# Seven products for eight in part of the down projection of a two-layer encoder kernel

## The chip, the cores and the metric

One core of a Trainium2 chip runs the kernel. The metric is the device time of one execution, in microseconds; three runs of the kernel before gave 2172.10, 2170.59 and 2173.06.

## What is computed

Two layers over 256 tokens of width 2048, in float32, and a final normalisation. Each layer has a token mixer and then a gated feed-forward block (the FFN), in which most of the time lies; the change is in the FFN alone.

```
def _conv_ffn(h, w_up, conv_w, conv_b, w_down):
    s = h.shape[1]
    up = h @ w_up
    padded = jnp.pad(up, ((0, 0), (CONV_WIDTH - 1, 0), (0, 0)))
    c = conv_b + sum(conv_w[j] * padded[:, j:j + s] for j in range(CONV_WIDTH))
    a, g = jnp.split(c, 2, axis=-1)
    return (jax.nn.silu(g) * a) @ w_down
```

`w_up` is 2048 x 11264 and `w_down` 5632 x 2048 in each layer.

## The kernel before

Every large product is made from float32 weights in three TensorE terms: a weight tile is split into a rounded part `hi` and a remainder `lo`, the activations likewise, and hi x hi, hi x lo and lo x hi are summed in PSUM. `load_split` (L240) does this for the weights. It loads 1 MB (four k-tiles of 128 x 512) into a `raw` tile by one DMA on SyncE's queue (L250), and then for each piece of 1024 columns (two k-tiles) ScalarE casts `hi` (L258) and VectorE subtracts to get `lo` (L259). There are three `raw` buffers and five each of `hi` and `lo`, so a piece can be prepared once TensorE has finished with the piece five before it.

The FFN (`ffn`, L384) goes through its 44 tiles of 128 hidden columns in groups of 8, 12, 12 and 12 (`GROUPS`, L30). In a group, for every four hidden tiles, `fm_panel` (L266) is run for the first half of the up projection and again for the gating half: 64 pairs of matmuls, one of 512 and one of 256 columns, into four PSUM banks. `branch` (L391) then forms the convolution of each of the four tiles: ScalarE L285, VectorE L286, GpSimd L287, ScalarE L401, VectorE L403 and L405. `gate` (L410) adds SiLU (ScalarE L413), the product with the first half (VectorE L414), and the split of the activation into `h` (ScalarE L416, GpSimd L417). Panels of the next weights run on TensorE while a branch or gate is worked off on the other engines.

After a group's panels `residual` (L321) multiplies its hidden tiles with the rows of `w_down` in four chunks n of 512 output columns. `tm_chunk` (L296) takes for each k-tile and each half of the tokens three matmuls of 512 columns (L292 to L294) into one PSUM bank per half; a group of 12 makes 72 matmuls a chunk. VectorE then adds both banks to the running `x_sb` (L326). In the last group of layer 1 the final two tiles are left to `final` (L332). The pools that matter: six PSUM banks `acc`, ten small tiles `w15`, six `m4`, six `k2`.

The order on each engine is set by a planner when the program is built: of the instructions that it takes to be ready, the one that stands first in the program goes first on its engine. On the chip each engine then runs its list in that order.

## Time and profile before

| | us |
|---|---|
| three runs, median | 2172.1 |
| profiled execution, its own time | 2171.22 |
| span of its profile, first to last instruction | 2169.4 |
| TensorE busy | 2155.6 (99%) |
| VectorE busy | 1428.6 (66%) |
| ScalarE busy | 1126.2 (52%) |
| GpSimd busy | 341.1 (16%) |

The span is what the hardware profiler saw of one execution; the time of that execution is 1.8 us longer, and lies between the lowest and the middle of the three runs. In the profile PE is TensorE (PEld its weight loads), DVE VectorE, ACT ScalarE, POOL GpSimd and SP SyncE. A matmul's record holds its whole passage through the array, so records overlap; the distance from start to start tells the rate. An idle time in brackets stands ahead of its instruction and names what ended it.

### The profile page before, as it was taken

Reading aid. Unit: us, or ns where it says so; the run is one execution under the profiler, and the core shown is the slowest. Engines: PE = TensorE matmul, PEld = TensorE weight load, DVE = VectorE, ACT = ScalarE, POOL = GpSimd, SP = SyncE. Lnnn points to the kernel's source line nnn. Section 1 sums busy time; section 2 is a strip of 40 time slices with the busy share of each in tenths; the row PEclk is TensorE's granted clock in tenths of the full one; section 3 lists DMA queues with packets and bytes.
Section 4 is the critical chain, followed back from the end, with each engine's and each line's share of the span. In section 5 each row is a group of like instructions: output and inputs, shape, how many; then the busy total and the mean of one; then the engine's idle time right before and its main releaser. Section 6 shows DMA issues by size and latency. Waiting matters only on the chain.

```text
span 2169.4 us, 29090 instructions
## 1 busy us (share of the span) xinstructions
PE 2155.6 (99%) x11301; PEld 1851.1 (85%) x11301; DVE 1428.6 (66%) x1796; ACT 1126.2 (52%) x1658; POOL 341.1 (16%) x537
## 2 busy tenths in 40 slices
PE   9999999999999999999999999999999999999998
PEld 7888888888888888888888888888888888888886
DVE  5655555687676578577756555558767758765875
ACT  6545545464554456355554445446545535544654
POOL 0110120031221033022103000002212202210320
PEclk9999999999999999999999999999999999999999
DMA  9655565556556555556655555555656655665553
GB/s 319 212 175 190 164 200 186 175 194 200 188 194 197 192 195 192 196 175 209 202 176 180 185 177 194 189 180 188 200 176 204 203 189 184 202 201 184 186 193 137
DMA packets 209965, 416.77 MB, mean 192 GB/s; under 512 B 7036, under 2 KB 10404, under 8 KB 209828
## 3 DMA queue, kind: packets, MB, share of 16 engines
q1 hardware_dynamic: 208676, 412.27, 57.6%
q10 hardware_dynamic: 1152, 2.65, 0.3%
q8 instruction: 88, 1.44, 0.3%
q14 instruction: 49, 0.40, 0.0%
HBM read 412.80 MB, written 2.89 MB: 192 GB/s over the span
## 4 chain that ended last, share of the span: by engine, by line
PE 98%; DMA 1%; DVE 0%; issue 0%; ACT 0%; SPq 0%; POOLq 0%; POOL 0%; DVEq 0%
PE fm_u L273 29%; PE fm_u L276 15%; PE tm_d L294 7%; PE tm_d L293 7%; PE tm_d L292 7%; PE tm_oab L292 1%; PE fm_kb L273 1%; PE tm_oab L294 1%; PE tm_oab L293 1%; PE tm_ocd L292 1%; PE tm_ocd L294 1%; PE tm_ocd L293 1%; PE fm_qa L273 1%; PE fm_qb L273 1%; PE fm_ka L273 1%; PE tm_va L292 1%
## 5 line engine op out<-in xcount | busy, mean ns | idle before, releaser
L259 DVE TENSOR_TENSOR lo<-raw,hi 128x1024 fp32r<-128x1024 f32 (+1 forms) x770 | 1009.4, 1328 | 589.0 <-ACT hi L258 584.8
L258 ACT CAST hi<-raw 128x1024 fp32r<-128x1024 f32 (+1 forms) x770 | 791.4, 1046 | 674.9 <-PE tm_d L294 205.2
L273 PE MATMUL fm_u<-x_n,hi 128*128 128x512 f32 x2816 | 958.8, 389 | 0.0
L276 PE MATMUL fm_u<-x_n,lo 128*128 128x256 f32 x2816 | 777.3, 276 | 0.0
L273 PEld LDWEIGHTS fm_u<-x_n,hi 128*128 128x128 f32 x2816 | 528.6, 188 | 110.0
L276 PEld LDWEIGHTS fm_u<-x_n,lo 128*128 128x128 f32 x2816 | 528.6, 188 | 0.4
L287 POOL TENSOR_TENSOR u<-hf_u,row_n 128x256 f32<-128x256 f32 x176 | 170.7, 970 | 920.9 <-DVE hf_u L286 913.3
L292 PE MATMUL tm_d<-hi,h 128*128 128x512 f32 x688 | 268.0, 390 | 0.0
L293 PE MATMUL tm_d<-lo,h 128*128 128x512 f32 x688 | 267.8, 389 | 0.0
L294 PE MATMUL tm_d<-hi,h 128*128 128x512 f32 x688 | 267.7, 389 | 0.0
L401 ACT ACTIVATE c<-u,conv 128x256 f32<-128x256 f32 x176 | 106.0, 602 | 206.5 <-POOL u L398 204.5
L294 PEld LDWEIGHTS tm_d<-hi,h 128*128 128x128 f32 x688 | 129.1, 188 | 26.9
L292 PEld LDWEIGHTS tm_d<-hi,h 128*128 128x128 f32 x688 | 129.2, 188 | 26.8
L293 PEld LDWEIGHTS tm_d<-lo,h 128*128 128x128 f32 x688 | 129.2, 188 | 26.5
L403 DVE SCALAR_TENSOR_TENSOR c<-u,conv,c 128x256 f32<-128x256 f32 x176 | 84.0, 477 | 71.8 <-ACT c L401 71.7
L417 POOL TENSOR_TENSOR h<-c,h 128x256 fp32r<-128x256 f32 x88 | 89.8, 1020 | 145.7 <-ACT h L416 145.7
L405 DVE SCALAR_TENSOR_TENSOR c<-u,conv,c 128x256 f32<-128x256 f32 x176 | 97.0, 551 | 0.3
L286 DVE TENSOR_TENSOR hf_u<-fm_u,hf_u 128x256 f32<-128x256 f32 x176 | 73.1, 415 | 0.0
L285 ACT COPY hf_u<-fm_u 128x256 f32<-128x256 f32 x176 | 62.8, 357 | 6.2 <-PE fm_u L276 3.1
L413 ACT ACTIVATE c<-c 128x256 f32<-128x256 f32 x88 | 36.7, 417 | 45.0 <-DVE c L405 44.5
L414 DVE TENSOR_TENSOR c<-c,c 128x256 f32<-128x256 f32 x88 | 48.5, 552 | 7.9 <-ACT c L413 7.8
L126 POOL TENSOR_TENSOR rstd_n<-s_n,mhalf 128x2 f32<-128x2 f32 x4 | 2.8, 695 | 306.9 <-DVE s_n L180 306.9
(277 smaller groups left out, 2373.4 us busy)
## 6 DMA issues: line engine op xcount, KB each, us to landing
raw<-in_ffn_w_up_dram SPq DMA_DIRECT2D x176, 1024.0 KB, 5.0
raw<-in_ffn_w_down_dram SPq DMA_DIRECT2D x86, 1024.0 KB, 5.1
raw<-in_ab_w_in_dram SPq DMA_DIRECT2D x47, 1024.0 KB, 5.1
raw<-in_cd_w_in_dram SPq DMA_DIRECT2D x40, 1024.0 KB, 5.1
raw<-in_ab_w_out_dram SPq DMA_DIRECT2D x16, 1024.0 KB, 5.1
raw<-in_cd_w_out_dram SPq DMA_DIRECT2D x16, 1024.0 KB, 5.1
x_sb<-in_x_dram SPq DMA_DIRECT2D x4, 512.0 KB, 12.4
raw<-in_ffn_w_down_dram SPq DMA_DIRECT2D x4, 512.0 KB, 3.8
```

The source lines that it names most:

```text
L258: nc.scalar.copy(hi[:, b:b + size], raw[:, j + b:j + b + size])
L259: nc.vector.tensor_tensor(lo[:, b:b + size], raw[:, j + b:j + b + size], hi[:, b:b + size].bitcast(F32), ALU.subtract)
L273: nc.tensor.matmul(banks[m], hi[k][:, m * P:(m + 1) * P], xr, start=(k0 + k == 0), stop=False, skip_group_check=True)
L276: nc.tensor.matmul(banks[m][:, :T], lo[k][:, m * P:(m + 1) * P], xr[:, :T], start=False, stop=(k0 + k == KT - 1), skip_group_check=True)
L287: nc.gpsimd.tensor_tensor(dst, half, row, ALU.mult)
L292: nc.tensor.matmul(bank, xh, hi, start=st, stop=False)
L293: nc.tensor.matmul(bank, xh, lo, start=False, stop=False)
L294: nc.tensor.matmul(bank, xl, hi, start=False, stop=sp)
L401: nc.scalar.activation(c, u[:, 2:], AF.Identity, bias=cb[:, fi:fi + 1], scale=w2[:, fi:fi + 1])
L403: nc.vector.scalar_tensor_tensor(c, u[:, 1:T + 1], w1[:, fi:fi + 1], c, ALU.mult, ALU.add)
L405: nc.vector.scalar_tensor_tensor(c, u[:, :T], w0[:, fi:fi + 1], c, ALU.mult, ALU.add)
L417: nc.gpsimd.tensor_tensor(h[:, 1, :], c, h[:, 0, :].bitcast(F32), ALU.subtract)
```

## The change

In `residual`, chunks 0, 2 and 3 of a group of 12 (all such groups but the last of layer 1: five groups, 15 chunks) are made by a new `down_chunk`. Its first and last four k-tiles are done as before. The middle four are two pairs of k-tiles; each pair, with both token halves and both halves of the 512 output columns, is a 2 x 2 block product, which `seven` makes from seven products of 256 columns instead of eight, by Strassen's scheme. The sums of weights it needs are made by `load_forms`: four VectorE sums over 512 elements, one in place and three into a second `raw` tile, then the split of 1024 and 768 columns per pair. The sums of activations are made once per group, by `pair_forms`, inside the gate of the group's second four tiles. The products are accumulated in the chunk's two banks and two more (`sums`), and `combine` adds those from `sums` to `x_sb`, by one ScalarE copy and seven VectorE operations. Chunk 1, groups of 8 and the last group stay with `tm_chunk`.

```diff
@@ -318,9 +318,98 @@
                         pump()
         return banks
 
-    def residual(w, parts, norm, name):
+    def load_forms(src):
+        cnt[0] += 1
+        i = cnt[0]
+        raw = wp.tile([P, 2048], F32, tag="raw", name=f"raw{i}")
+        more = wp.tile([P, 2048], F32, tag="raw", name=f"more{i}")
+        nc.sync.dma_start(
+            raw.rearrange("p (k f) -> p k f", k=4), src.rearrange("(k p) f -> p k f", p=P))
+        v = raw.rearrange("p (q j n c) -> p q j n c", q=2, j=2, n=2)
+        b11, b12, b21, b22 = (v[:, :, j, n] for j in range(2) for n in range(2))
+        t3, t2, t4 = (
+            more[:, :1536].rearrange("p (q f c) -> p q f c", q=2, f=3)[:, :, f] for f in range(3))
+        nc.vector.tensor_tensor(t3, b12, b22, ALU.add)
+        nc.vector.tensor_tensor(b12, b11, b12, ALU.add)
+        nc.vector.tensor_tensor(t2, b12, b22, ALU.add)
+        nc.vector.tensor_tensor(t4, t2, b21, ALU.add)
+        quads = []
+        for q in range(2):
+            forms = []
+            for j, (part, m) in enumerate(((raw, 1024), (more, 768))):
+                hi = wp.tile([P, 1152], F32R, tag="hi", name=f"hi{i}_{q}{j}", bufs=5)[:, :m]
+                lo = wp.tile([P, 1024], F32R, tag="lo", name=f"lo{i}_{q}{j}", bufs=5)[:, :m]
+                pv = part[:, q * m:(q + 1) * m]
+                nc.scalar.copy(hi, pv)
+                nc.vector.tensor_tensor(lo, pv, hi.bitcast(F32), ALU.subtract)
+                forms += [(hi[:, b:b + 256], lo[:, b:b + 256]) for b in range(0, m, 256)]
+            quads.append(forms)
+        return quads
+
+    def seven(banks, sums, xs, rs, forms, first, last):
+        rh, rl = rs
+        a11, a21 = ((xs[0][:, 0, t * P:(t + 1) * P], xs[0][:, 1, t * P:(t + 1) * P]) for t in range(2))
+        a12, a22 = ((xs[1][:, 0, t * P:(t + 1) * P], xs[1][:, 1, t * P:(t + 1) * P]) for t in range(2))
+        r5, r6, r7, r3 = ((rh[:, f * P:(f + 1) * P], rl[:, f * P:(f + 1) * P]) for f in range(4))
+        b11, t1, b21, b22, t3, t2, t4 = forms
+        for dst, (ah, al), (bh, bl), own in (
+                (sums[0][:, :256], a11, b11, True), (sums[1][:, :256], r5, t1, True),
+                (banks[0][:, :256], a12, b21, False), (banks[0][:, 256:], r3, b22, False),
+                (sums[1][:, 256:], r7, t3, False), (sums[0][:, 256:], r6, t2, False),
+                (banks[1][:, :256], a22, t4, False)):
+            nc.tensor.matmul(dst, ah, bh, start=own and first, stop=False, skip_group_check=True)
+            nc.tensor.matmul(dst, ah, bl, start=False, stop=False, skip_group_check=True)
+            nc.tensor.matmul(dst, al, bh, start=False, stop=last, skip_group_check=True)
+
+    def combine(sums, n, name):
+        c = n * 512
+        x11, x21 = (x_sb[:, t, c:c + 256] for t in range(2))
+        p1 = w15(f"p1_{name}", 256)
+        nc.scalar.copy(p1, sums[0][:, :256])
+        w = w15(f"pw_{name}", 256)
+        nc.vector.tensor_tensor(w, sums[0][:, 256:], p1, ALU.subtract)
+        e = w15(f"pe_{name}", 256)
+        nc.vector.tensor_tensor(e, sums[1][:, :256], w, ALU.add)
+        nc.vector.tensor_tensor(x11, x11, p1, ALU.add)
+        nc.vector.tensor_tensor(x21, x21, w, ALU.subtract)
+        nc.vector.tensor_tensor(x21, x21, sums[1][:, 256:], ALU.subtract)
+        xb = x_sb[:, :, c + 256:c + 512]
+        nc.vector.tensor_tensor(xb, xb, e.unsqueeze(1).to_broadcast([P, 2, 256]), ALU.add)
+        nc.vector.tensor_tensor(xb[:, 1], xb[:, 1], sums[1][:, 256:], ALU.add)
+
+    def down_chunk(w, r0, xs, nk, rs, n, name):
+        banks = [acc(f"tm_{name}{t}") for t in range(2)]
+        sums = [acc(f"tms_{name}{t}") for t in range(2)]
+        for k0 in range(0, nk, 4):
+            kn = min(4, nk - k0)
+            src = w[r0 + k0 * P:r0 + (k0 + kn) * P, n * 512:n * 512 + 512]
+            if k0 == 4:
+                quads = load_forms(src)
+                for q in range(2):
+                    k = k0 + 2 * q
+                    seven(banks, sums, xs[k:k + 2], rs[q], quads[q], q == 0, q == 1)
+                    pump()
+                combine(sums, n, name)
+                continue
+            hi, lo = load_split(src, kn)
+            for k in range(kn):
+                a = xs[k0 + k]
+                for t in range(2):
+                    xh, xl = (a[:, j, t * P:(t + 1) * P] for j in range(2))
+                    for j, (s, m) in enumerate(((xh, hi[k]), (xh, lo[k]), (xl, hi[k]))):
+                        nc.tensor.matmul(
+                            banks[t], s, m, start=k0 + k + j == 0, stop=False, skip_group_check=True)
+                if k % 2 == 1:
+                    pump()
+        return banks
+
+    def residual(w, parts, norm, name, rs=None):
         for n in range(4):
-            banks = tm_chunk(w, parts, n * 512, f"{name}{n}")
+            if not rs or n == 1:
+                banks = tm_chunk(w, parts, n * 512, f"{name}{n}")
+            else:
+                (r0, xs, nk), = parts
+                banks = down_chunk(w, r0, xs, nk, rs, n, f"{name}{n}")
             for t in range(2):
                 xc = x_sb[:, t, n * 512:(n + 1) * 512]
                 nc.vector.tensor_tensor(xc, banks[t], xc, ALU.add)
@@ -407,32 +496,49 @@
                 cs.append(c)
                 yield m, c
 
-        def gate(kt0, cs, banks):
+        def pair_forms(c0, c1, nm):
+            r = m4(f"r{nm}")[:, :512]
+            r5, r6, r7, r3 = (r[:, f * P:(f + 1) * P] for f in range(4))
+            nc.vector.tensor_tensor(r5, c0[:, P:], c1[:, P:], ALU.subtract)
+            nc.vector.tensor_tensor(r6, c0[:, :P], r5, ALU.subtract)
+            nc.vector.tensor_tensor(r7, c0[:, P:], c0[:, :P], ALU.subtract)
+            nc.vector.tensor_tensor(r3, c1[:, :P], r6, ALU.subtract)
+            rh, rl = (
+                kp.tile([P, 512], F32R, tag="k2", name=f"r{j}{nm}", bufs=6) for j in range(2))
+            nc.scalar.copy(rh, r)
+            nc.vector.tensor_tensor(rl, r, rh.bitcast(F32), ALU.subtract)
+            return rh, rl
+
+        def gate(kt0, cs, banks, rs=None):
             nm = f"{layer}_{kt0}"
+            prev = None
             for m, c in branch(kt0, 1, banks):
                 nc.scalar.activation(c, c, AF.Silu)
                 nc.vector.tensor_tensor(c, cs[m], c, ALU.mult)
                 h = act(f"h{m}{nm}")
                 nc.scalar.copy(h[:, 0, :], c)
                 nc.gpsimd.tensor_tensor(h[:, 1, :], c, h[:, 0, :].bitcast(F32), ALU.subtract)
+                if rs is not None and m % 2 == 1:
+                    rs.append(pair_forms(prev, c, f"{nm}{m}"))
+                prev = c
                 yield h
 
         f0 = 0
         early = None
         for gi, gs in enumerate(GROUPS):
-            hs = []
+            hs, rs = [], []
             last = gi == len(GROUPS) - 1
             for kt0 in range(f0, f0 + gs, 4):
                 cs = early or [c for _, c in branch(kt0, 0, panel(kt0, 0))]
                 early = None
-                hs += gate(kt0, cs, panel(kt0, 1))
+                hs += gate(kt0, cs, panel(kt0, 1), rs if gs == 12 and not (last and nxt is None) and kt0 == f0 + 4 else None)
             if gs < 12:
                 early = [c for _, c in branch(f0 + gs, 0, panel(f0 + gs, 0))]
             if last and nxt is None:
                 residual(down, ((f0 * P, hs, gs - 2),), None, f"d{layer}{gi}")
                 final(down, (f0 + gs - 2) * P, hs[gs - 2:])
             else:
-                residual(down, ((f0 * P, hs, gs),), nxt if last else None, f"d{layer}{gi}")
+                residual(down, ((f0 * P, hs, gs),), nxt if last else None, f"d{layer}{gi}", rs)
             f0 += gs
 
     def heads_to_act(src, hd, name):
```

## Rows read from the trace of the kernel before

**Rows 1.** The page: each engine's busy time, and slices of the span.

```profile
PE 2155.6 (99%) x11301; PEld 1851.1 (85%) x11301; DVE 1428.6 (66%) x1796; ACT 1126.2 (52%) x1658; POOL 341.1 (16%) x537
...
PEclk9999999999999999999999999999999999999999
```

**Rows 2.** The page, part 4: the chain that ended last, by engine.

```profile
PE 98%; DMA 1%; DVE 0%; issue 0%; ACT 0%; SPq 0%; POOLq 0%; POOL 0%; DVEq 0%
```

**Rows 3.** Windows: stretch, length; busy PE, PEld, DVE, ACT, POOL; clock, DMA, GB/s.

```profile
632.41:654.18 21.77, 21.77 (x131) 19.26 (x129) 15.99 (x23) 11.76 (x17) 3.62 (x8) 1.00 0.63 207
654.18:670.50 16.32, 16.32 (x74) 13.52 (x73) 14.83 (x20) 11.35 (x20) 7.94 (x10) 1.00 0.52 168
670.50:686.82 16.32, 16.32 (x73) 13.51 (x73) 10.01 (x11) 6.33 (x6) 0.00 (x0) 1.00 0.70 238
686.82:703.14 16.32, 16.32 (x73) 13.51 (x73) 8.55 (x9) 6.33 (x6) 0.00 (x0) 1.00 0.59 193
703.14:719.50 16.36, 16.36 (x73) 13.52 (x73) 8.60 (x9) 6.31 (x6) 0.00 (x0) 1.00 0.58 193
```

**Rows 4.** Timeline, TensorE, 256-wide matmuls of the last chunk: start, duration.

```profile
2158.49 0.28 PE L293 MATMUL fin<-lo,h 128*128 128x256 f32 x1
...
2158.97 0.28 PE L294 MATMUL fin<-hi,h 128*128 128x256 f32 x1
...
2160.74 0.28 PE L293 MATMUL fin<-lo,h 128*128 128x256 f32 x1
...
2161.21 0.28 PE L294 MATMUL fin<-hi,h 128*128 128x256 f32 x1
```

**Rows 5.** Groups by form: line, shapes, count | busy us, mean ns | idle.

```profile
L730 DVE TENSOR_TENSOR kcs<-kcs,kcr 128x512 f32<-128x512 f32 x2 | 1.3, 682 | 0.0
...
L185 DVE TENSOR_SCALAR dg_n<-ident,rstd_n 128x128 f32<-128x128 f32 x2 | 0.5, 283 | 0.8 <-POOL u L398 0.8
...
L258 ACT CAST hi<-raw 128x1024 fp32r<-128x1024 f32 x766 | 789.2, 1048 | 674.9 <-PE tm_d L294 205.2 <-PE fm_u L273 183.5 <-PE tm_oab L294 44.5
...
L286 DVE TENSOR_TENSOR hf_u<-fm_u,hf_u 128x256 f32<-128x256 f32 x176 | 73.1, 415 | 0.0
L285 ACT COPY hf_u<-fm_u 128x256 f32<-128x256 f32 x176 | 62.8, 357 | 6.2 <-PE fm_u L276 3.1
...
L326 DVE TENSOR_TENSOR x_sb<-tm_d,x_sb 128x512 f32<-128x512 f32 x64 | 41.0, 682 | 0.0
...
L416 ACT CAST h<-c 128x256 fp32r<-128x256 f32 x88 | 35.5, 404 | 17.2 <-DVE c L414 16.5
```

**Rows 6.** Timeline, VectorE, panel before and chunk 0; idle in brackets.

```profile
649.23 2.36 DVE L259 TENSOR_TENSOR lo<-raw,hi 128x1024 fp32r<-128x1024 f32 x2 [3.03 <-ACT hi L258]
...
657.70 3.45 DVE L259 TENSOR_TENSOR lo<-raw,hi 128x1024 fp32r<-128x1024 f32 x2
...
662.53 1.76 DVE L259 TENSOR_TENSOR lo<-raw,hi 128x1024 fp32r<-128x1024 f32 x1
...
666.00 1.77 DVE L259 TENSOR_TENSOR lo<-raw,hi 128x1024 fp32r<-128x1024 f32 x1
...
669.53 2.36 DVE L259 TENSOR_TENSOR lo<-raw,hi 128x1024 fp32r<-128x1024 f32 x2 [1.42 <-ACT hi L258]
```

**Rows 7.** Timeline, VectorE, a remainder in chunk 2.

```profile
690.87 1.23 DVE L259 TENSOR_TENSOR lo<-raw,hi 128x1024 fp32r<-128x1024 f32 x1 [1.49 <-ACT hi L258]
```

**Rows 8.** The page, part 6: DMA issues, size, microseconds to landing.

```profile
raw<-in_ffn_w_down_dram SPq DMA_DIRECT2D x86, 1024.0 KB, 5.1
```

**Rows 9.** Timeline, panel after the second gate: VectorE, then TensorE.

```profile
623.76 0.43 DVE L414 TENSOR_TENSOR c<-c,c 128x256 f32<-128x256 f32 x1 [0.49 <-ACT c L413]
625.61 4.64 DVE L259 TENSOR_TENSOR lo<-raw,hi 128x1024 fp32r<-128x1024 f32 x4 [1.42 <-ACT hi L258]
...
627.66 0.39 PE L273 MATMUL fm_u<-x_n,hi 128*128 128x512 f32 x1
```

## The prediction

> **What bounds the kernel now.** I read the page first. TensorE is busy for 99% of the span, at a granted clock of nine tenths or more in every slice [rows 1], that is its 2.4 GHz level, and it holds 98% of the chain that ended last [rows 2]. So time is saved only by taking work off TensorE, and lost wherever TensorE is made to wait. VectorE is at 66% over the span, but that mean hides what matters here, so I cut one cycle of the first FFN into stretches [rows 3]: the last up-projection panel of a group of 12, then the four down-projection chunks. TensorE is full in all five. VectorE is busy for 16.0 us of 21.8, then 14.8 of 16.3 in chunk 0 (the gate of that last panel still runs beside it), 10.0 in chunk 1, and 8.6 in chunks 2 and 3. Chunk 0 has no VectorE time to give; chunks 2 and 3 have nearly half.
>
> **What it takes off TensorE.** A quarter-chunk that is changed had 4 k-tiles x 2 row halves x 3 = 24 matmuls of 512 columns. A chunk of 72 takes 16.32 us [rows 3], 0.2267 us each, so 24 take 5.44 us. In their place stand 2 x 7 x 3 = 42 matmuls of 256 columns, each with its own weight load. By columns alone (half of 0.2267 us) they would take 4.76 us. But the trace has such a run, the 256-wide matmuls of the last chunk: (2158.97 - 2158.49)/4 = 0.120 us and (2161.21 - 2160.74)/4 = 0.1175 us from start to start [rows 4]. At 0.119 us, 42 take 5.00 us. The saving is 0.44 us a chunk; 15 chunks (n = 0, 2, 3 in the five groups of 12 that qualify) make **6.6 us**. The bounds are 0.40 us at 0.120 (6.0 us in all) and 0.68 us at the rate of columns (10.2 us); I take the measured run because it has the same width and load for load.
>
> The Trainium skill ("TensorE: Matmul & The Clock Gate", section "Back-to-back issue gap") gives 262 cycles at 2.4 GHz for 256 columns and 518 for 512, 0.109 and 0.216 us. By it the saving would be 24 x 0.216 - 42 x 0.109 = 0.60 us a chunk, 9.0 us in all, as an estimate. The rows differ from it in both widths, 0.119 and 0.2267 us, so the rows decide.
>
> **What it adds to VectorE.** Per changed chunk: four sums of 512 elements at 0.68 (the SBUF add of that size [rows 5]), 2.7 us. Two more remainders of 768 elements, between 0.68 for 512 and 1.23 for 1024 (a pair takes 2.36 [rows 6]), so 0.96 each, 1.9 us. The combining: six operations on 256 elements at 0.415 and one on 512 at 0.68 [rows 5], 3.2 us. Together **7.8 us**. ScalarE gets two casts of 768, 0.83 us each on the line between 0.40 for 256 and 1.05 for 1024, and one copy of 0.36 [rows 5], 2.0 us a chunk; it has 5 us of room in chunk 0 and 10 elsewhere [rows 3], so its own time costs nothing, only its place in the queue does. Per group, two pairs of activations add four subtractions of 128 (bounded by 0.28 for a one-input operation of that size and 0.415 for 256; I take 0.28, the same size) and one remainder of 0.68, 1.8 us each. PSUM holds (six banks, four in use by a changed chunk), and no load is added: still three of 1 MB per chunk.
>
> **Chunks 2 and 3: hidden.** 8.6 + 7.8 = 16.4 us of VectorE work against 15.9 us of TensorE work (16.3 less 0.44). That is 0.5 us over per chunk. What covers it is the lead of the split: with five buffers a remainder is made as soon as TensorE frees the piece five before, so it may be four pieces of 12 matmuls (10.9 us) early, less 1.05 for the cast and 1.23 for itself, some 8.5 us; VectorE idles 1.49 us ahead of each [rows 7]. An overrun of 1.0 us in two chunks fits. Chunk 1, unchanged, has 6 us free to catch up in. The scratch tile takes one of three raw buffers, so loads start later; a load lands 5.1 us after issue [rows 8]. The load for chunk 1 can start when the changed quarter's fourth remainder is done, at about 5.3 us into chunk 0 (657.70 and 1.7 more, less 654.18), and lands at 10.4, ahead of the 15.9 at which it is used. I cost it at nothing.
>
> **Chunk 0: not hidden.** Count from its start at 654.18. The remainders, one buffer piece each, end as follows before: the sixth piece at 6.97 (657.70 + 3.45), the seventh at 10.1, the eighth at 13.6, then a pair that ends at 17.7, the first of it at about 16.6 [rows 6]. After the change the chunk has eight pieces, not six, and TensorE asks for the seventh at 5.44 + 5.00 = 10.44, the eighth at 13.16, the ninth (chunk 1's first) at 15.88 and the tenth at 18.60. In the old order and with nothing added, their margins are +0.3, -0.4, -0.7 and +0.9 us. Two of the pieces ahead of the seventh are now 768 wide and take 0.27 less each: +0.9, +0.1, -0.2, +1.4. The four sums can go ahead of the crunch, into the 3.03 us that VectorE idles in the panel before [rows 6]; this cover is just wide enough, and if the load of that piece is late the 2.7 us fall into the crunch. What is left is the combining, 3.2 us, which can start at 10.44, and stands in the program ahead of the remainders of chunk 1. Placed before the ninth piece it makes that 3.4 us late, or 2.0 if it fills the 1.42 us that VectorE idles there [rows 6]; behind the ninth but before the tenth, 1.8 or 0.4; behind both, 0. I take the middle, **1.6 us** a group, bounds 0 and 3.4.
>
> **The pair sums.** They fall in the panel that follows the second gate of the group. There VectorE has idles of 0.49 and 1.42 us, and the remainder at the end of the gate (625.61 + 1.23 = 626.84) is used by the matmul at 627.66: 0.8 us to spare [rows 9]. The first pair brings 1.8 us ahead of it, the second may bring its four subtractions, 1.1 us. If the idles take all of it the cost is 0; if none, 1.8 + 1.1 - 0.8 = 2.1 us. I take **0.4**, near the lower end, because 1.9 us of idle lie in that very stretch.
>
> **Sum.** Given back: (1.6 + 0.4) x 5 = 10 us. Net +3.4 us. The profiled execution took 2171.2 us against a median of 2172.1, 0.04% apart, so the same step holds for both: 2174.6 and **2175.5**. A measurement of this kernel can tell about 0.2%, 4.3 us, from no change.
>
> **Rivals.** (a) *The waits stay within the lead.* If the combining is put behind the remainders of chunk 1's first pieces and the pair sums fall into idle time, not more than 0.4 us a group is lost and nearly all of the 6.6 us stays: 2165.5 to 2167.5. For it: the margins are around zero, not far below, and VectorE has idle time on both sides of each crunch. Against it: program order puts the combining first. With the column rate, 10.2 us, it would be 2162. (b) *VectorE becomes the bound through the first chunk of every group.* From the panel before through chunk 0 its work is 16.0 + 14.8 + 7.8 = 38.6 us in 21.8 + 15.9 = 37.7 us, more than TensorE's, with waits for the gate's own chain that cannot all be filled. If the sums too fall into chunk 0, or the combining goes ahead of the ninth piece, 3 us or more are lost a group; at 3.6, 18 - 6.6 = +11.4 us, 2183.5, and at the sum of the upper bounds, 3.4 + 2.1 = 5.5, 2193. It decides against the change from 1.3 us a group on. For it: remainders that take 1.23 us in chunks where GpSimd rests take 1.76 in chunk 0, where it works too [rows 3, 6, 7]. Against it: chunk 1 has the slack to end any queue, so the loss cannot spread beyond one place in a cycle.
>
> **How the numbers follow.** Forecast (1.4 to 3.0 us lost a group, 2172.5 to 2180.5): 0.40, half of it within 0.2% and half above. Rival (a): 0.34. Between them (0.4 to 1.4 us): 0.08, within 0.2%. Rival (b), over 3.0 us: 0.18. So faster 0.34, same 0.28, slower 0.38. The range goes from 2164.5, which takes in (a) and some of the column rate, to 2186, which takes in half of (b).
>
> **What would show it.** TensorE: 270 more matmuls, groups of 256 columns 0.119 us apart; 0.113 would mean the higher gain. VectorE busy some 135 us more (15 x 7.8 + 5 x 3.6). TensorE's idle time, next to nothing before in the FFN, should stand in chunk 0 of five groups, at the matmuls just behind the changed quarter, waiting for a remainder, with the combining just ahead of it on VectorE; none in chunks 2 and 3. Waits in chunks 2 and 3 would make the lead argument wrong; no waits at all would make rival (a) right.

## The result, and where the time went

| | before | after |
|---|---|---|
| median | 2171.53 us (4 runs) | 2184.31 us (4 runs, 2181.77 to 2186.76) |
| ratio | | 1.0058, interval 1.0045 to 1.007 |
| span of the profiled execution | 2169.4 us | 2182.6 us |

The change makes the kernel 0.58% slower. The forecast was 2175.5 us, range 2164.5 to 2186. The time lies inside that range because the range took in half of rival (b): it is near that rival's 2183.5 us, and came about by that rival's mechanism more than by the forecast's.

The page of the kernel after, parts 1 and 4, the lines that answer to [rows 1, 2]:

```profile
PE 2154.4 (99%) x11571; PEld 1860.5 (85%) x11571; DVE 1547.4 (71%) x2041; ACT 1156.8 (53%) x1713; POOL 340.1 (16%) x537
...
PE 85%; DVE 9%; issue 2%; DMA 1%; POOL 1%; ACT 1%; SPq 0%; POOLq 0%; DVEq 0%; ACTq 0%
```

TensorE has the 270 more matmuls, and its busy time hardly changed (2155.6 before), though 6 us of work are gone: a busy record can stretch over a wait (16.46 us of busy time below, in a chunk with 15.89 us of work). The chain tells more. Before, TensorE held 98% of it; now VectorE holds 9%: there are places at which TensorE waits for VectorE.

The windows of the first group of 12 in the kernel after: the panel before, then chunks 0 to 3; columns as in [rows 3].

```profile
633.58:655.35 21.77, 21.77 (x130) 19.32 (x129) 18.91 (x26) 11.25 (x16) 3.94 (x9) 1.00 0.46 149
...
655.35:674.40 19.05, 16.46 (x92) 14.05 (x91) 17.92 (x26) 14.53 (x25) 7.71 (x12) 1.00 0.63 214
674.40:690.72 16.32, 16.32 (x73) 13.51 (x72) 14.37 (x19) 6.11 (x6) 0.00 (x0) 1.00 0.47 157
690.72:706.61 15.89, 15.89 (x92) 13.99 (x90) 11.75 (x18) 6.36 (x7) 0.00 (x0) 1.00 0.49 173
706.61:722.49 15.88, 15.88 (x91) 13.99 (x90) 14.05 (x21) 9.23 (x11) 0.00 (x0) 1.00 0.73 253
```

Read against [rows 3], the answer stands in the first column. The panel is as long as before (21.77 us). Chunks 2 and 3 are 0.43 us shorter (16.32 to 15.89), TensorE full in both. Chunk 0, which should have become 15.89 too, is 19.05 us: **3.16 us lost in one place**. VectorE is busy for 17.92 of the 19.05 us. The same count, from the first matmul of a chunk to the first of the next, over all five groups:

| | chunk 0 | chunk 1 | chunks 2 and 3 |
|---|---|---|---|
| before | 16.34 to 16.38 | 16.32 (third group 17.21) | 16.32 (third group 17.25 and 17.22) |
| after | 19.05, 19.14, 19.06, 20.85, 19.06 | 16.32 (third group 18.32) | 15.89 (third group 16.78 and 16.82) |
| sum of the differences | +15.3 | +1.1 | -4.3 |

Together +12.1 of the 13.2 us between the spans. The rest is lost before the first FFN begins (at 391.64 us before, 392.82 after). The kernels below have the same start, and in their profiles the FFN begins anywhere between 391.3 and 393.6 us, so this part goes with the execution more than with the change.

TensorE's timeline in chunk 0, the changed quarter's second pair and the matmul behind it:

```profile
664.61 0.28 PE L362 MATMUL tm_d<-hi,r 128*128 128x256 f32 x1
664.73 0.28 PE L360 MATMUL tms_d<-hi,r 128*128 128x256 f32 x1
666.10 0.39 PE L361 MATMUL tms_d<-lo,r 128*128 128x256 f32 x1 [1.08 <-DVE lo L344]
...
667.15 0.40 PE L400 MATMUL tm_d<-hi,h 128*128 128x512 f32 x1
669.05 0.50 PE L400 MATMUL tm_d<-lo,h 128*128 128x512 f32 x1 [1.50 <-DVE lo L259]
```

Two waits: 666.10 - 664.73 less the 0.12 of a step, 1.25 us, for the last remainder of the changed quarter, and 669.05 - 667.15 less 0.23, 1.67 us, for the first remainder behind it. Steps of 256 columns are 0.12 us apart (664.61 to 664.73), as in [rows 4].

VectorE's timeline in the same stretch; it answers to [rows 6]:

```profile
649.47 0.69 DVE L332 TENSOR_TENSOR more<-raw 128x512 f32<-128x512 f32 x1 [0.74 <-DMA raw<-in_ffn_w_down_dram]
...
651.65 0.69 DVE L335 TENSOR_TENSOR more<-more,raw 128x512 f32<-128x512 f32 x1
652.26 1.22 DVE L259 TENSOR_TENSOR lo<-raw,hi 128x1024 fp32r<-128x1024 f32 x1
653.40 1.22 DVE L344 TENSOR_TENSOR lo<-raw,hi 128x1024 fp32r<-128x1024 f32 x1
654.53 0.42 DVE L286 TENSOR_TENSOR hf_u<-fm_u,hf_u 128x256 f32<-128x256 f32 x1
...
664.56 1.48 DVE L344 TENSOR_TENSOR lo<-more,hi 128x768 fp32r<-128x768 f32 x1
...
667.21 2.92 DVE L259 TENSOR_TENSOR lo<-raw,hi 128x1024 fp32r<-128x1024 f32 x2
...
670.38 2.90 DVE L259 TENSOR_TENSOR lo<-raw,hi 128x1024 fp32r<-128x1024 f32 x2
673.21 0.41 DVE L370 TENSOR_TENSOR pw_d<-tms_d,p_d 128x256 f32<-128x256 f32 x1
...
675.47 0.41 DVE L378 TENSOR_TENSOR x_sb<-x_sb,tms_d 128x256 f32<-128x256 f32 x1
```

Read it from the bottom. The combining (673.21 to 675.9) comes after both remainders that TensorE waited for, and after three more: it is not what holds them up. Then the top: VectorE stands idle for 0.74 us until the load of the changed quarter lands, makes the four sums, and only then the two remainders and, at 654.53, the first operation of the gate. The sums sit right ahead of the crunch, and everything behind them is late. Now the load itself. SyncE's queue in the kernel before, the second load of chunk 0:

```profile
640.59 0.37 SPq L250 DMA_DIRECT2D raw<-in_ffn_w_down_dram  x1
```

And the same load in the kernel after:

```profile
644.34 0.37 SPq L326 DMA_DIRECT2D raw<-in_ffn_w_down_dram  x1
```

Before, it was issued 13.6 us ahead of that chunk (654.18 - 640.59), after it is 11.0 us (655.35 - 644.34). A load waits for a free buffer, and a buffer is free when its remainders are made. So I went back to where remainders first fall behind, in the panel that follows the second gate; VectorE, after:

```profile
630.68 0.69 DVE L509 TENSOR_TENSOR r<-r,r 128x512 fp32r<-128x512 f32 x1 [0.69 <-ACT r L508]
631.63 2.36 DVE L259 TENSOR_TENSOR lo<-raw,hi 128x1024 fp32r<-128x1024 f32 x2 [0.26 <-ACT hi L258]
```

In [rows 9] the last of four remainders ends at 630.25 (625.61 + 4.64), 23.9 us ahead of chunk 0; now the last one stands behind the second pair sum's split and ends at 633.99, 21.4 us ahead: 2.5 us later, and the loads are 2.6 us later from there to chunk 0. That panel loses nothing on TensorE (the up-projection stretches last 108.81 and 130.57 us in both kernels); the price of the pair sums is paid two panels on. This was the theory to be tested: **the pair sums delay remainders, these the loads, the late load puts the weight sums right ahead of the crunch in chunk 0.**

### The profile page after: what moved, and what is told of

Same layout as the page of the kernel before. It is cut to its first block, busy times and chain, and to the rows that moved or that the text cites. A ratio compares the mean times of both kernels' runs of the same rounds, so it can differ in the third digit from the quotient of the medians.

```text
span 2182.6 us, 30008 instructions
## 1 busy us (share of the span) xinstructions
PE 2154.4 (99%) x11571; PEld 1860.5 (85%) x11571; DVE 1547.4 (71%) x2041; ACT 1156.8 (53%) x1713; POOL 340.1 (16%) x537
## 4 chain that ended last, share of the span: by engine, by line
PE 85%; DVE 9%; issue 2%; DMA 1%; POOL 1%; ACT 1%; SPq 0%; POOLq 0%; DVEq 0%; ACTq 0%
PE fm_u L273 23%; PE fm_u L276 11%; PE tm_d L400 6%; PE tm_d L292 3%; PE tm_d L293 3%; PE tm_d L294 3%; DVE lo L259 3%; PE tm_oab L292 1%; PE fm_kb L273 1%; PE tm_oab L294 1%; PE tm_ocd L292 1%; PE tm_ocd L294 1%; PE tm_oab L293 1%; PE tm_ocd L293 1%; PE fm_qa L273 1%
## 5 line engine op out<-in xcount | busy, mean ns | idle before, releaser
L259 DVE TENSOR_TENSOR lo<-raw,hi 128x1024 fp32r<-128x1024 f32 (+1 forms) x740 | 961.3, 1320 | 449.5 <-ACT hi L258 445.5
L258 ACT CAST hi<-raw 128x1024 fp32r<-128x1024 f32 (+1 forms) x740 | 759.0, 1046 | 568.5 <-PE fm_u L273 162.8
L287 POOL TENSOR_TENSOR u<-hf_u,row_n 128x256 f32<-128x256 f32 x176 | 165.7, 942 | 922.3 <-DVE hf_u L286 916.2
L400 PE MATMUL tm_d<-hi,h 128*128 128x512 f32 x480 | 154.0, 393 | 0.0
L292 PE MATMUL tm_d<-hi,h 128*128 128x512 f32 x328 | 127.7, 389 | 0.0
L293 PE MATMUL tm_d<-lo,h 128*128 128x512 f32 x328 | 127.6, 389 | 0.0
L294 PE MATMUL tm_d<-hi,h 128*128 128x512 f32 x328 | 127.6, 389 | 0.0
L520 POOL TENSOR_TENSOR h<-c,h 128x256 fp32r<-128x256 f32 x88 | 90.1, 1024 | 159.1 <-ACT h L519 159.1
L400 PEld LDWEIGHTS tm_d<-hi,h 128*128 128x128 f32 x480 | 90.9, 189 | 18.6
L400 PE MATMUL tm_d<-lo,h 128*128 128x512 f32 x240 | 94.7, 395 | 7.5 <-DVE lo L259 7.5
L294 PEld LDWEIGHTS tm_d<-hi,h 128*128 128x128 f32 x328 | 61.6, 188 | 12.8
L292 PEld LDWEIGHTS tm_d<-hi,h 128*128 128x128 f32 x328 | 61.6, 188 | 12.8
L293 PEld LDWEIGHTS tm_d<-lo,h 128*128 128x128 f32 x328 | 61.6, 188 | 12.6
```

The source lines that it names most:

```text
L258: nc.scalar.copy(hi[:, b:b + size], raw[:, j + b:j + b + size])
L259: nc.vector.tensor_tensor(lo[:, b:b + size], raw[:, j + b:j + b + size], hi[:, b:b + size].bitcast(F32), ALU.subtract)
L287: nc.gpsimd.tensor_tensor(dst, half, row, ALU.mult)
L292: nc.tensor.matmul(bank, xh, hi, start=st, stop=False)
L293: nc.tensor.matmul(bank, xh, lo, start=False, stop=False)
L294: nc.tensor.matmul(bank, xl, hi, start=False, stop=sp)
```

## The experiments

Times are medians with the ratio to the kernel before and its interval; "chunk 0" lists the five groups.

| run | us | ratio | chunk 0, us |
|---|---|---|---|
| chunks 2 and 3 only | 2168.88 | 0.9987 (0.9977 to 0.9996) | 16.37, 16.37, 16.38, 16.37, 16.81 |
| own scratch | 2184.81 | 1.0059 (1.0044 to 1.0074) | 19.02, 19.08, 19.26, 18.50, 19.13 |
| no pair sums | 2175.45 | 1.0017 (1.0008 to 1.0026) | 16.66, 17.82, 16.64, 16.63, 16.65 |
| no sums in chunk 0 | 2172.47 | 1.0004 (0.9994 to 1.0013) | 16.66, 17.22, 16.64, 16.69, 16.66 |
| no combining in chunk 0 | 2186.68 | 1.0066 (1.005 to 1.0082) | 19.05, 22.05, 20.60, 21.84, 20.68 |
| pair sums on GpSimd | 2195.27 | 1.0112 (1.0097 to 1.0126) | 21.06, 21.90, 22.36, 22.54, 22.57 |
| sums of chunk 0 on GpSimd | 2199.67 | 1.013 (1.0115 to 1.0144) | 23.01, 23.17, 22.80, 22.75, 22.72 |
| chunks 1, 2, 3 | 2170.89 | 0.9998 (0.9989 to 1.0007) | 16.68, 16.67, 16.68, 16.68, 16.69 |
| pair sums early | 2171.98 | 1.0007 (0.9998 to 1.0016) | 17.22, 18.03, 17.22, 16.65, 17.22 |
| quarter last in chunk 0 | 2192.48 | 1.01 (1.0085 to 1.0116) | 21.96, 20.42, 21.98, 20.55, 22.00 |
| early, and last | 2193.52 | 1.0102 (1.0089 to 1.0116) | 21.97, 20.44, 21.98, 21.99, 20.40 |
| late chunks of all groups | 2171.81 | 1.0006 (0.9997 to 1.0015) | 16.37, 16.35, 16.37, 16.36, 16.38 |

**Chunks 2 and 3 only.**

```diff
-            if not rs or n == 1:
+            if not rs or n not in (2, 3):
```

> The seven products stay in chunks 2 and 3; chunk 0 goes back to the plain product (10 chunks instead of 15). Theory A (the time is lost in chunk 0 alone, because VectorE is late there while the gate still runs): no waits of TensorE in the FFN, 10 x 0.44 us saved, so 2171.5 - 4.4 = 2167.1 us. Rival B (the pair sums, or VectorE work as such, make TensorE wait): waits of 1 us or more a group stay, 2172 us or more.

Measured 2168.88 us, 0.13% faster than before and the fastest of all kernels here. Its windows, chunks 0 to 3 of the first group:

```profile
656.09:672.46 16.37, 16.37 (x74) 13.52 (x73) 14.87 (x20) 11.37 (x20) 7.96 (x10) 1.00 0.54 174
672.46:688.78 16.32, 16.32 (x73) 13.51 (x72) 12.49 (x15) 6.10 (x6) 0.00 (x0) 1.00 0.49 167
688.78:704.67 15.89, 15.89 (x92) 13.99 (x90) 12.01 (x18) 6.52 (x8) 0.00 (x0) 1.00 0.36 132
704.67:720.55 15.88, 15.88 (x91) 13.99 (x90) 13.63 (x20) 8.55 (x10) 0.00 (x0) 1.00 0.75 259
```

TensorE is full in all four, and each changed chunk is 0.43 us shorter. Ten of them are 4.3 us; the median moved by 2.3. In the profiled execution the FFN began 1.9 us later than in the profile of before, which is most of the difference there. That delay arises in the first 25 us of the span, ahead of everything that was changed: there the granted clock stood at 0.50 for 3.4 us, as in the profile after the change and not in that of before. Whether this is the whole of it is open; another profile with such a stretch starts its FFN at 391.7 us. The pair sums are still made and the load of that quarter is as late as after the change (issued 11.0 us ahead of chunk 0); with no weight sums in chunk 0, nothing waits for it. So the loss hangs on chunk 0 alone, and lateness only hurts where there are sums behind it.

**Own scratch.** The scratch tile of the weight sums no longer takes a load buffer.

```diff
-        more = wp.tile([P, 2048], F32, tag="raw", name=f"more{i}")
+        more = kp.tile([P, 1536], F32, tag="big6", name=f"more{i}")
```

> As the changed kernel, with the scratch tile of the weight sums in a buffer of its own instead of one of the three load buffers. Theory C (the load of the changed quarter lands too late because the scratch takes a load buffer, and the sums then fall into the gate): the load of chunk 0's changed quarter lands 3 us sooner or more, the sums start before the gate, and most of the 3.0 us of waiting a group goes: 2166 to 2172 us. Theory A without C (VectorE has simply too much to do in chunk 0): at most 1 us a group comes back, 2179 us or more.

No difference, 2184.81 us. The next loads do go out earlier (7.7 us ahead of chunk 0 in place of 1.8), but the load of the changed quarter itself does not (11.0 us ahead, as after the change), and the waits stay. The taken load buffer is not the cause here.

**No pair sums.** The activations' own split stands in for their sums, so the pair sums and their split are left out.

```diff
-        r5, r6, r7, r3 = ((rh[:, f * P:(f + 1) * P], rl[:, f * P:(f + 1) * P]) for f in range(4))
+        r5, r6, r7, r3 = ((z[:, 0, t * P:(t + 1) * P], z[:, 1, t * P:(t + 1) * P]) for z in rs for t in range(2))
...
-                    rs.append(pair_forms(prev, c, f"{nm}{m}"))
-                prev = c
+                    rs.append((prev, h))
+                prev = h
```

> The four sums of activations and their split are left out; other activations of the same shape stand in their place in the products. Rival B (the pair sums make VectorE late, either in their own panel or by delaying the loads behind it): the load of chunk 0's changed quarter lands some 2.5 us sooner, and 2 us or more of waiting a group go, 2174 us or less. Theory A: within 2 us of the changed kernel, 2182 to 2186 us.

2175.45 us, above the 2174 us or less that were expected, but chunk 0 falls from 19.1 to 16.65 us in four groups (17.82 in the second), and the load of the changed quarter goes out 13.6 us ahead again: work done two panels earlier decides a wait in chunk 0. The median says less than the chunks, because one stretch elsewhere became slower: the first panels of layer 1 took 103.79 us for 100.85 (last section).

**No sums in chunk 0.** The four weight sums of chunk 0 are left out; its products take the weights as loaded.

```diff
-    def load_forms(src):
+    def load_forms(src, sums=True):
...
-        more = wp.tile([P, 2048], F32, tag="raw", name=f"more{i}")
+        more = wp.tile([P, 2048], F32, tag="raw", name=f"more{i}") if sums else raw
...
-                quads = load_forms(src)
+                quads = load_forms(src, n != 0)
```

> In chunk 0 alone the four sums of weights are left out, and the second piece of each pair is split from the loaded tile once more, so that the scratch tile goes too; casts, remainders, matmuls and the combining stay. Theory A or C: 2.9 us of VectorE work and the buffer are gone from the crunch, waits fall to 0.5 us a group or less, 2166 to 2169 us. If the combining or the extra remainders are what makes VectorE late: 2 us or more of waiting a group stay, 2178 us or more.

2172.47 us, above the 2166 to 2169 us that were expected: 2.4 us of the 3.16 come back per group, and chunk 0 stays 0.75 us longer than 15.89. Even without the 2.9 us of sums, two more remainders in the crunch cost something. Taking away either block, pair sums or weight sums, gives back nearly the same 2.4 us: the two are not added up, they meet in one chain.

**No combining in chunk 0.** The eight operations of the combining are left out there.

```diff
-                combine(sums, n, name)
+                if n != 0:
+                    combine(sums, n, name)
```

> The changed kernel with the combining (one ScalarE copy, seven VectorE operations) left out in chunk 0 of each group; the products are still made. The forecast's account, in which the combining stands ahead of a remainder that TensorE waits for: the waits in chunk 0 fall by 1.6 us a group or more, 2174 to 2177 us. The backlog theory, in which VectorE is behind before the changed quarter and the combining comes later than the waits: the waits stay at 2.7 to 3.1 us a group, 2182 to 2185 us.

2186.68 us: chunk 0 gives nothing back. VectorE's timeline shows the same remainders at the same distance, with the combining gone behind them:

```profile
666.70 2.91 DVE L259 TENSOR_TENSOR lo<-raw,hi 128x1024 fp32r<-128x1024 f32 x2
...
669.87 5.17 DVE L259 TENSOR_TENSOR lo<-raw,hi 128x1024 fp32r<-128x1024 f32 x4
```

And TensorE's timeline shows the same first wait:

```profile
665.58 0.39 PE L361 MATMUL tms_d<-lo,r 128*128 128x256 f32 x1 [1.09 <-DVE lo L344]
```

The forecast's own account, the combining's place, falls for chunk 0. (Four groups are even longer than after the change; their waits are the same 2.9 to 3.3 us, and the rest is the clock, see the last section.)

**Pair sums on GpSimd.** One of the four lines:

```diff
-            nc.vector.tensor_tensor(r5, c0[:, P:], c1[:, P:], ALU.subtract)
+            nc.gpsimd.tensor_tensor(r5, c0[:, P:], c1[:, P:], ALU.subtract)
```

> The changed kernel with the eight subtractions of activations per group made on GpSimd instead of VectorE; nothing is left out. They are about 2.2 us of the 3.6 us that the pair sums put on VectorE. Backlog theory, the sum of VectorE's work from the panel before through chunk 0 decides: the waits in chunk 0 fall from 3.05 us to 0.8 to 1.8 us a group, 2173 to 2178 us. Rival, in which GpSimd's work slows VectorE's remainders or delays the split of the activations so that nothing is won: 2182 to 2187 us. A third way, in which only the place of one late load counts and the sum does not: no change, 2184 us, with the load of the changed quarter issued as late as before, 11.0 us ahead of chunk 0.

2195.27 us, above all three branches. VectorE has eight operations less, and the load of the changed quarter is issued not earlier but later, 10.5 us ahead of chunk 0 (at 654.44); SyncE's queue:

```profile
643.94 0.37 SPq L326 DMA_DIRECT2D raw<-in_ffn_w_down_dram  x1
```

because the split of the sums stays on VectorE, in its old place ahead of the remainders, and VectorE stands there for 1.56 us until GpSimd and ScalarE have delivered (VectorE's timeline):

```profile
629.16 0.69 DVE L509 TENSOR_TENSOR r<-r,r 128x512 fp32r<-128x512 f32 x1 [1.56 <-ACT r L508]
630.10 3.50 DVE L259 TENSOR_TENSOR lo<-raw,hi 128x1024 fp32r<-128x1024 f32 x3 [0.25 <-ACT hi L258]
```

Most of the 11 us above the change is the clock, which fell in all five groups (last section); what bears on the question is the first wait. VectorE's work went down, the load became 0.5 us later, and that wait grew by 0.6 us (1.25 to 1.83). So the time of the load counts and not VectorE's total; that GpSimd's own work adds to the wait is not excluded by this run. Less work on an engine does not help where its queue still stops at the same place.

**Sums of chunk 0 on GpSimd.** The four additions of `load_forms` go to GpSimd for n = 0, one line of four:

```diff
-        nc.vector.tensor_tensor(t3, b12, b22, ALU.add)
+        eng.tensor_tensor(t3, b12, b22, ALU.add)
...
-                quads = load_forms(src)
+                quads = load_forms(src, nc.gpsimd if n == 0 else None)
```

> The changed kernel with the four sums of weights of chunk 0 made on GpSimd; nothing is left out. Backlog theory: 2.7 us leave VectorE's queue; if GpSimd makes the four sums within some 5 us of the load's landing (about 6 us ahead of chunk 0), the waits fall to 0.6 to 1.2 us a group as where the sums were left out, 2172 to 2176 us. If GpSimd is much slower than VectorE at them, over 2 us each, the changed quarter is itself late and the waits grow: 2185 to 2200 us.

2199.67 us, the upper branch, though only two of the four sums take over 2 us. GpSimd's timeline:

```profile
648.37 1.30 POOL L333 TENSOR_TENSOR more<-raw 128x512 f32<-128x512 f32 x1 [6.21 <-DVE lo L259]
649.74 2.15 POOL L334 TENSOR_TENSOR raw<-raw 128x512 f32<-128x512 f32 x1
651.98 1.30 POOL L335 TENSOR_TENSOR more<-raw 128x512 f32<-128x512 f32 x1
653.36 2.15 POOL L336 TENSOR_TENSOR more<-more,raw 128x512 f32<-128x512 f32 x1
```

7.1 us in place of VectorE's 2.9, so the changed quarter itself is late, and GpSimd starts the gate's part late too. The clock fell in all five groups here as well.

**Chunks 1, 2 and 3.**

```diff
-            if not rs or n == 1:
+            if not rs or n not in (1, 2, 3):
```

> The seven products in chunks 1, 2 and 3 instead of 0, 2 and 3; nothing is left out. Backlog theory: chunk 0 has no sums of weights and stays without waits as in the kernel that changes chunks 2 and 3 alone; 15 chunks save 0.43 us each, 6.4 us, and three changed chunks in a row overrun TensorE by some 0.5 us each, which the lead of 8.5 us takes: 2164.5 to 2167 us, faster than both. Rival, in which without a free chunk VectorE does not catch up after chunk 0 and the waits move to chunks 1 and 2: 2169 to 2176 us.

2170.89 us, no measurable gain: the rival, with the waits one chunk later than it said. Chunk 0 is nearly free of waits (16.68), but with no unchanged chunk behind it, VectorE does not catch up. The last two of the windows, chunks 2 and 3 of the first group:

```profile
686.83:703.22 16.39, 16.29 (x91) 14.11 (x90) 14.80 (x21) 7.84 (x9) 0.00 (x0) 1.00 0.55 192
703.22:719.49 16.27, 16.10 (x91) 13.95 (x90) 15.73 (x22) 8.36 (x10) 0.00 (x0) 1.00 0.66 228
```

Both should be 15.89; VectorE is at 15.73 of 16.27. The lead that hides two changed chunks does not hide three.

**Pair sums early.** The pair sums move to the gate of the group's first four hidden tiles, two panels earlier; those k-tiles are then the changed ones, still the second quarter of a chunk.

```diff
-        for k0 in range(0, nk, 4):
+        for k0 in (4, 0, 8):
...
-            if k0 == 4:
+            if k0 == 0:
...
-                            banks[t], s, m, start=k0 + k + j == 0, stop=False, skip_group_check=True)
+                            banks[t], s, m, start=k0 == 4 and k + j == 0, stop=False, skip_group_check=True)
...
-                hs += gate(kt0, cs, panel(kt0, 1), rs if gs == 12 and not (last and nxt is None) and kt0 == f0 + 4 else None)
+                hs += gate(kt0, cs, panel(kt0, 1), rs if gs == 12 and not (last and nxt is None) and kt0 == f0 else None)
```

> The changed kernel with the pair sums made in the gate of the group's first four hidden tiles, two panels earlier, and so with the seven products on those four k-tiles; they are still the second quarter of a chunk (order 4, 0, 8). Nothing is left out. Late-load theory (the pair sums stand ahead of remainders in their panel, these free the load buffers, and so the load of the changed quarter is issued 11.0 us ahead of chunk 0 and not 13.6, which sets when its sums can start): two panels more let the loads recover, the issue goes back to 13.6 us ahead, the waits in chunk 0 fall from 3.05 to 0.5 to 1.0 us a group, 2172 to 2176 us. Rival, the total of VectorE's work around chunk 0 decides, whatever the time of the load: no change, 2182 to 2186 us.

2171.98 us, 12 us less than the change with the same arithmetic; in the profiles 10.8 us of this stand in chunk 0, 1.8 of them because the clock fell in no group. The load of the changed quarter on SyncE's queue:

```profile
640.82 0.37 SPq L326 DMA_DIRECT2D raw<-in_ffn_w_down_dram  x1
```

654.41 - 640.82 = 13.6 us ahead, as before the change, and chunk 0 is 17.22 us or less in four groups of five (18.03 in the second). VectorE is as full as after the change, in the panel before and in chunk 0 (windows):

```profile
632.64:654.41 21.77, 21.77 (x130) 19.26 (x129) 18.67 (x27) 11.76 (x17) 3.62 (x8) 1.00 0.49 156
654.41:671.63 17.22, 16.21 (x92) 13.99 (x91) 17.18 (x25) 13.23 (x23) 7.25 (x10) 1.00 0.60 201
```

18.67 and 17.18 us against 18.91 and 17.92: the sum of the work did not go away, its place did. That settles the late load as the cause of the larger part, 1.8 us of the 3.16 in the first group; the 0.76 to 1.33 us that stay in these four groups (2.14 in the second) are the crunch itself, and they eat the saving of chunk 0.

**Quarter last in chunk 0**, and then this together with the early pair sums.

```diff
-        for k0 in range(0, nk, 4):
+        for k0 in (0, 8, 4) if n == 0 else range(0, nk, 4):
```

> The changed kernel with the changed quarter made as the last of chunk 0 (order 0, 8, 4); the other chunks as they are; nothing is left out. The sums of weights then need not be ready until 10.9 us into chunk 0, and the load can be late. If the waits come from the place of the sums ahead of the gate and of the first remainders: they fall to 0 to 1.5 us a group, 2167 to 2177 us. If VectorE's total through chunk 0 is what does not fit, the waits only move to the end of chunk 0 or the start of chunk 1: 2179 to 2186 us.

> Both moves together: pair sums two panels earlier, and the changed quarter last in chunk 0 and second in chunks 2 and 3. Nothing is left out. If late loads and the place of the sums make up the waits, nearly none is left: 15 chunks at 0.43 us, 2165 to 2169 us, at or below the kernel that changes chunks 2 and 3 alone (2168.9 us). If VectorE's total decides, 0.5 us or more a group stays: 2170 to 2178 us.

2192.48 and 2193.52 us: both outside everything expected. The second run has in chunk 0 the order 4, 8, 0. TensorE's timeline in the first shows what went wrong:

```profile
662.73 0.50 PE L400 MATMUL tm_d<-hi,h 128*128 128x512 f32 x1 [1.10 <-ACT h L519]
...
666.01 0.50 PE L400 MATMUL tm_d<-hi,h 128*128 128x512 f32 x1 [1.29 <-ACT h L519]
```

Those waits are for activations, not for weights. The third quarter's hidden tiles come from the last gate, which runs beside chunk 0, and I had moved that quarter forward. The order of the quarters is set by when the gate delivers; what the place of the changed quarter alone would do is left open by these runs.

**Late chunks of all groups.** Chunks 2 and 3 of the groups of 12 and of layer 1's last group, and chunk 3 of the groups of 8.

```diff
-            if not rs or n == 1:
+            if not rs or n not in ((2, 3) if parts[0][2] > 8 else (3,)):
...
-                hs += gate(kt0, cs, panel(kt0, 1), rs if gs == 12 and not (last and nxt is None) and kt0 == f0 + 4 else None)
+                hs += gate(kt0, cs, panel(kt0, 1), rs if kt0 == f0 + 4 else None)
...
-                residual(down, ((f0 * P, hs, gs - 2),), None, f"d{layer}{gi}")
+                residual(down, ((f0 * P, hs, gs - 2),), None, f"d{layer}{gi}", rs)
```

> The seven products only where VectorE has idle time: chunks 2 and 3 of the five groups of 12 as in the kernel that changes those alone, and besides them chunks 2 and 3 of the last group of layer 1 (ten k-tiles) and chunk 3 of the two groups of 8. Nothing is left out. 14 chunks at 0.43 us are 6.0 us, 1.7 us more than the ten of that kernel: 2166 to 2168 us, no waits in the FFN. Rival, the shorter chunks of these groups (10.9 and 13.6 us against VectorE's 6.0 and 7.3 us, with 7.8 added) do not take the work: waits of 0.5 us or more in them or in the panel that follows, and no gain, 2168.5 to 2172 us.

2171.81 us, no gain, and the sum hides two opposite parts. The two groups of 8 went from 43.55 to 43.09 us each, without a wait: right. The last group went from 54.43 to 55.96, and the rest of the span behind it from 20.5 to 23.6. TensorE's timeline where `final` begins, and the window behind it:

```profile
2145.16 0.73 PE L292 MATMUL fin<-hi,h 128*128 128x512 f32 x2 [1.70 <-ACT hi L258]
2146.42 0.50 PE L293 MATMUL fin<-lo,h 128*128 128x512 f32 x1 [0.53 <-DVE lo L259]
```

```profile
2147.40:2150.80 3.40, 3.40 (x9) 2.64 (x9) 3.24 (x5) 1.31 (x3) 0.00 (x0) 0.50 0.01 2
```

`final` waits 2.2 us, and right behind it TensorE runs for 3.4 us at half the clock. What it waits for is again a late load. SyncE's queue with the two loads of `final`, in the kernel before:

```profile
2129.64 5.81 SPq L250 DMA_DIRECT2D raw<-in_ffn_w_down_dram  x2
```

And in this one, with ScalarE's casts behind them:

```profile
2137.58 1.24 SPq L250 DMA_DIRECT2D raw<-in_ffn_w_down_dram  x2
...
2144.06 1.99 ACT L258 CAST hi<-raw 128x1024 fp32r<-128x1024 f32 x2 [3.30 <-DMA raw<-in_ffn_w_down_dram]
```

Before, the first was issued 19.2 us ahead of `final` (2148.86), here 7.6 us ahead (2145.16). The two go out at 2137.58 and 2138.45, when VectorE is done with the last remainder of chunk 3's loaded tile (2137.56) and of its scratch tile (2138.42). Here the scratch tile in a load buffer does cost something; a run with a scratch tile of its own was not made for this version. The version that the runs point to, chunks 2 and 3 of the groups of 12 and chunk 3 of the groups of 8, was not run; as an estimate from these stretches (twice 0.46) it would save 0.9 us more than chunks 2 and 3 only.

## Why the prediction came out as it did

- **The saving** was sized at 0.44 us a chunk from the measured 256-wide spacing [rows 4], and is 0.43 (16.32 to 15.89). The Trainium skill ("TensorE: Matmul & The Clock Gate", "Back-to-back issue gap") would have given 0.60, as an estimate; the chunks of this trace do not agree with it.
- **VectorE's work**: 135 us forecast, 118.8 came (1547.4 - 1428.6). The single prices hold where GpSimd rests (0.69 for a sum, 0.95 for a remainder of 768; beside GpSimd 1.48), and the durations of all VectorE records add up to 140.7 us more (1519.6 before, 1660.2 after). But short operations in a row start before the one ahead has ended: the combining's seven take 2.7 us (673.21 to 675.9) and not the 3.2 us that the durations add up to.
- **Chunks 2 and 3 hidden**: right, shown in the run that changes those alone. The lead has a limit, shown by chunks 1, 2 and 3.
- **Chunk 0, 1.6 us a group**: this is the step that failed. I let the four sums disappear in the 3.03 us that VectorE idles in the panel before [rows 6], with the remark that they fall into the crunch if the load is late, and then made the whole loss out of the combining's place. The load was late (11.0 us ahead of the chunk, not 13.6), the sums did fall there, and in chunk 0 the combining stood behind every remainder that mattered. Measured: 3.16 us in the first group, 3.2 in three more, 4.96 in one. The waits did come in the chunk that was named, but one of the two inside the changed quarter, and neither with the combining ahead of it.
- **The pair sums, 0.4 us in their own panel**: wrong in kind. They cost that panel nothing. They delay its remainders by 2.5 us, and with them every load up to chunk 0. I priced them by their neighbours on TensorE and did not ask which buffers, and so which loads, wait for the remainders that they are put ahead of.
- **"The loss cannot spread beyond one place in a cycle"**, said against rival (b): not quite. In the third group chunk 1 holds the next layer's norm, and grew from 17.21 to 18.32 us; there TensorE's transposes wait for `x_sb`, which VectorE adds up late, with the combining just ahead (1068.73 to 1071.41). How much of the 1.1 us is the combining's is not shown: in the run without it this chunk takes 17.25 us, but the clock fell in that group's chunk 0, and where it did so with the combining in place the chunk takes 17.21 to 17.27 us too.

```profile
1073.20 0.33 PE L161 MATMUL xt_n<-ident,x_sb 128*128 128x128 f32 x1 [0.39 <-DVE x_sb L415]
```

- **The scratch tile**, costed at nothing although it holds a load buffer: right for this change, shown by the run that takes it elsewhere, and not for the last group, where `final` waits for the buffer.
- **Rival (b)** had the mechanism in words (VectorE over its limit from the panel before through chunk 0, with the sums in chunk 0) and at 3.6 us a group its 2183.5 us is 0.8 from the result. That nearness is in part luck: the mean of the five chunks 0 is 3.5 us over 15.89 only with the group in which the clock fell, and the start and the third group's chunk 1, 2.3 us together, stood in no rival's sum. Of its two conditions the sums in chunk 0 came true, the combining ahead of the ninth piece did not. It argued from the total of the work; the run with early pair sums shows that the same total in another place costs 12 us less.
- **The sum** on the profiled executions: forecast +3.4 us, measured +13.2. Of the 9.8 between them, chunk 0 holds some 7.8 (five times the difference of 3.16 and 1.6), the clock in one group 1.8, the third group's chunk 1 1.1 and the start 1.2; the 2 us put down for the pair sums did not come.

## What to carry over

An instruction put ahead of a buffer's last reader costs twice: its own time where it stands, and the delay of the next load into that buffer, which may surface panels later where there is no slack. So follow each inserted operation to the buffers behind it in its queue, and place extra work where the chunk's window shows idle time on its engine (chunks 2 and 3 here) rather than spreading it evenly. A move of work to another engine helps only if the wait moves too.

## What the runs showed of the hardware

**The clock follows the waits.** The windows of the fourth group after the change, with chunk 0's two waits in the first line; the last columns are granted clock, DMA share and GB/s:

```profile
1719.80:1724.50 4.70, 1.92 (x13) 1.40 (x12) 4.66 (x7) 4.37 (x7) 1.45 (x2) 1.00 0.83 295
1724.50:1728.00 3.50, 3.50 (x9) 2.75 (x10) 3.50 (x4) 2.77 (x5) 1.31 (x2) 0.51 0.73 238
```

TensorE was busy for 1.92 of 4.70 us, and then ran at 0.51 of its clock, the 1.2 GHz level, for 3.5 us. That makes this chunk 0 20.85 us long where the other groups have 19.06: 1.8 us more for the same wait. Over the profiles, in the kernels whose chunk 0 stays at or under 18.03 us the clock never fell there. With waits of 2.4 to 3.3 us it fell in one group of five after the change, in none with a scratch tile of its own, in four without the combining; with the longer waits of the two GpSimd runs in all five. The length of the waits does not decide it alone: with some 4.1 to 4.4 us of them, in four pieces, in the two runs with the quarter last, it fell in three groups of five. Nor does the kernel decide it: of the four executions of the changed kernel the slowest (2186.76 us) shows a mean clock of 0.995, the fastest (2181.77 us) one of 0.998. Where the clock falls, a group loses 1.5 to 3 us on top of the wait. No term of the forecast had this.

**GpSimd and VectorE take turns.** Of GpSimd's four sums in the run that gives it the sums of chunk 0, two take 1.30 and two 2.15 us, though all have the same size and two inputs. VectorE's remainders beside them, in the same stretch:

```profile
649.27 1.48 DVE L259 TENSOR_TENSOR lo<-raw,hi 128x1024 fp32r<-128x1024 f32 x1 [1.66 <-ACT hi L258]
653.02 1.35 DVE L345 TENSOR_TENSOR lo<-raw,hi 128x1024 fp32r<-128x1024 f32 x1 [2.27 <-ACT hi L344]
```

The first begins while GpSimd makes its first sum (648.37 to 649.67) and ends 1.08 us after that sum; the second sum ends 1.15 us after this remainder. It is the same at both places in all five groups: the remainders last 1.33 to 2.01 us, in place of 1.22, and each ends 1.08 to 1.09 us after the sum that was under way, and the sum behind it 1.14 to 1.15 us after the remainder. The Trainium skill ("SBUF — State Buffer", "Who interferes with whom") says that a VectorE operation with both inputs in SBUF and a GpSimd operation that reads SBUF block each other, whichever starts first going ahead. These rows agree with it.

**A stretch 3% slower with nothing waiting.** In two kernels (no pair sums, no combining in chunk 0) the 592 matmuls of layer 1's first panels took 103.79 us in place of 100.85, at a granted clock of 1.00 and with TensorE busy throughout; in all others it was 100.85. The code of these panels is the same. The cause is open.
